# Two encoder layers on one core: the feed-forward of blocks 0 and 1 from group 8 on as seven products in place of eight, block 2 by itself

## The chip, the cores and the metric

The kernel is one program on one core of a Trainium2 chip. The core has five engines with a queue each, run in order: TensorE (PE: matmuls, with a second unit PEld that loads the weights of the next one), VectorE (DVE), ScalarE (ACT), GpSimd (POOL) and SyncE (SP), which here only issues DMAs. [...] The metric is the device time of one execution in microseconds (us): 2456.24 us in the median of three runs of the kernel before (2454.12 to 2459.05).

## The reference

Two layers of a streaming encoder on 1024 prompt tokens and 8 x 16 sample tokens, width 1024, all float32:

```python
for l in range(DEPTH):                       # 2 layers; prompt and sample tokens alike
    h = rms_norm(x, norm1_g[l])
    q, k, v, u = project(h, w_in[l], ...)    # u = a * sigmoid(b)
    a_o = attention in a window, with sinks  # 8 heads of 64, 2 kv heads
    c_o = silu(layer_norm(depthwise conv31(u)))
    x = x + concatenate([a_o * beta_a, c_o * beta_c]) @ w_out[l]
    h = rms_norm(x, norm2_g[l])
    x = x + square(relu(h @ w_up[l])) @ w_down[l]     # 1024 -> 4096 -> 1024
```

The last line is the feed-forward, and the change is in it.

## The kernel before, in words

**Blocks and products.** The 1152 tokens are three blocks of 384 columns. An activation x is held as 8 tiles of [128, 384] (features by tokens). Every product is done in float32r with both operands split into a high and a low part: of (w_hi + w_lo)(h_hi + h_lo) three of the four terms are summed, so a [1024, 128] weight unit times a block is 8 x 3 = 24 matmuls of 384 columns (`gemm`, L193 to L195). `half_unit` (L184 to L186) prepares half of a unit: a DMA of 256 KB into a `raw` buffer (4 of these), ScalarE casts the high part, and GpSimd subtracts it from the raw to get the low part; `w` has 6 buffers. A "step" below is 24 matmuls.

**Feed-forward.** The 4096 hidden features are 16 groups of 256. For a group and a block, "up" is 2 units, and `hidden` (L667 to L670) turns each of their results into relu, square, a high part (all three on ScalarE) and a low part (VectorE, L670). "Down" multiplies these by the group's rows of w_down: 8 results of [128, 384], 6 matmuls each (L686), each added to x by VectorE (L688). So a group costs one block 96 matmuls: 4 steps. `feed_forward` runs groups over several blocks, sharing the prepared weights; `feed_one` runs one block by itself, two groups at a time.

**The order of the work.** The program is traced in one order, and that order is the priority of the instructions for a list scheduler at build time: each engine's queue is fixed by it before the kernel runs. `side` streams (convolution, attention) give out a step or so beside each unit (`tick`), and one background stream `self.back` gives `mix` steps beside each unit (`unit_done`, `fill`); `flush` runs the rest of it.

**A layer.** After the projections, attention and convolution of the blocks, the order at the end of a layer (L833 to L850) is: groups up to `place` for blocks 0 and 1 in the foreground; then `out(2)` (the output projection of block 2, 8 units, and its norm) with groups `place` to `join` of blocks 0 and 1 as background; then the rest. In layer 0 `place` is 8 and `join` 16: blocks 0 and 1 do groups 8 to 15 beside and behind `out(2)`, and block 2 does all its 16 groups alone, as the background of layer 1's projections. In layer 1 `place` is 7 and `join` 8: from group 8 on the three blocks go together, and then block 2 does groups 0 to 7 alone at the very end. When a block's last group is done, its x is stored to DRAM and, in layer 0, its norm for layer 1 is computed (`stored`, `rmsnorm`, L230 to L248). Layer 1 begins with three background steps, then the first projection, which needs the norm of block 0.

**Buffers.** `big` has 9 slots of [128, 8 x 384] float32 for x, the two parts of h, the attention and convolution results and the like (`slot`, L77). PSUM: 3 banks `g` for products, 2 for the scores `s`, one each of `m`, `r` and `c`. `tmp` has 8 buffers of [128, 384].

The lines that matter most, by the profile's numbers: L184 to L186 weight preparation, L193 to L195 unit products, L212 to L248 the norm, L667 to L670 `hidden`, L686 and L688 `down`, L838 to L850 the end of a layer.

## Time and profile before

| | before |
|---|---|
| median of 3 runs | 2456.24 us |
| profiled execution, span | 2455.0 us |
| TensorE matmuls | 14206, busy 2397.7 us (98%) |
| VectorE | 2821 instructions, busy 1494.7 us (61%) |
| ScalarE | 2444, busy 1130.4 us (46%) |
| GpSimd | 1007, busy 1236.0 us (50%) |
| weight loads (`raw`) | 792 of 256 KB |

The profile is of one execution; its span runs from its first to its last instruction, and 2455.0 us is that execution's own time as the profile gives it, 1.2 us under the median of the timed runs. "Busy" of TensorE counts matmuls that overlap in a pipeline, so a matmul's own duration (0.34 us) is longer than the distance from its start to the next one's. A busy share is a mean over stages: VectorE is nearly always busy in the first 560 us, and has much idle time in the stages that the change touches. The time between an instruction's end and the next on its engine is laid to what released it ("<-").

### The profile page before, as it was taken

To read this page: it belongs to the slowest core of one execution; us is meant where nothing else is said; L and a number is where in the kernel's file an instruction comes from. 1 tells how busy PE (TensorE), PEld (TensorE's weight loads), DVE (VectorE), ACT (ScalarE), POOL (GpSimd) and SP (SyncE) were. 2 spreads that over 40 slices of the span, in tenths; PEclk is the share of its full clock that TensorE was granted. 3 is DMA by queue.
4 is the path that set the end of the run, shared out by engine and by line. 5 is a ranking of instruction groups with operands and counts; after the bars stand their busy time and mean duration, and the time that the engine had idled before them with its cause. 6 is when DMAs were issued, how large, how long until landed. Compare 5 with 4: busy or idle time off the path is not lost.

```text
span 2455.0 us, 38647 instructions
## 1 busy us (share of the span) xinstructions
PE 2397.7 (98%) x14206; PEld 2346.3 (96%) x14206; DVE 1494.7 (61%) x2821; ACT 1130.4 (46%) x2444; POOL 1236.0 (50%) x1007
## 2 busy tenths in 40 slices
PE   6999999999999999999999999999999999999999
PEld 6899888999999999999999999899999999999999
DVE  6999988996324333787777754889832433333322
ACT  5467545655333233544664566456433322222342
POOL 6875575566343233767755856756424422221363
PEclk9899999999999999999999999999999999999999
DMA  5423423333322222443333434334222211111342
GB/s 186 139 82 98 124 94 113 108 105 118 97 86 74 65 69 91 142 131 108 117 110 108 131 117 131 123 96 124 80 88 86 87 43 44 44 44 35 112 138 77
DMA packets 169692, 243.39 MB, mean 99 GB/s; under 512 B 23536, under 2 KB 70896, under 8 KB 169456
## 3 DMA queue, kind: packets, MB, share of 16 engines
q1 hardware_dynamic: 169504, 240.94, 31.4%
q8 instruction: 111, 1.82, 0.3%
q14 instruction: 77, 0.63, 0.1%
HBM read 230.27 MB, written 12.90 MB: 99 GB/s over the span
## 4 chain that ended last, share of the span: by engine, by line
PE 78%; DVE 15%; issue 2%; POOL 2%; ACT 2%; DMA 0%; SPq 0%; POOLq 0%; ACTq 0%; DVEq 0%
PE g L686 19%; PE g L193 15%; PE g L195 15%; PE g L194 15%; DVE c L318 6%; PE m L686 4%; PE r L686 4%; PE c L686 3%; PE s L496 1%; POOL w L186 1%; PE m L531 1%; DVE h L248 1%; DVE f L246 1%; DVE s L212 1%; DVE x L688 1%
## 5 line engine op out<-in xcount | busy, mean ns | idle before, releaser
L186 POOL TENSOR_TENSOR w<-raw,w 128x512 fp32r<-128x512 f32 x792 | 1051.6, 1339 | 1098.0 <-ACT w L185 1078.5
L185 ACT CAST w<-raw 128x512 fp32r<-128x512 f32 x792 | 483.1, 619 | 594.2 <-PE g L686 221.7
L193 PE MATMUL g<-h,w 128*128 128x384 f32 x2208 | 747.5, 339 | 7.1 <-ACT h L247 3.5
L195 PE MATMUL g<-h,w 128*128 128x384 f32 x2208 | 747.6, 339 | 0.0
L194 PE MATMUL g<-h,w 128*128 128x384 f32 x2208 | 746.1, 338 | 0.0
L686 PE MATMUL g<-hid,w 128*128 128x384 f32 x3072 | 566.1, 340 | 11.0 <-DVE x L688 8.4
L686 PEld LDWEIGHTS g<-hid,w 128*128 128x128 f32 x3072 | 535.2, 189 | 17.3 <-DVE x L688 10.4
L318 DVE SCALAR_TENSOR_TENSOR c<-u,vec,c 128x384 f32<-128x384 f32 (+1 forms) x960 | 498.0, 519 | 18.0
L193 PEld LDWEIGHTS g<-h,w 128*128 128x128 f32 x2208 | 417.4, 189 | 11.1 <-ACT h L247 4.3
L194 PEld LDWEIGHTS g<-h,w 128*128 128x128 f32 x2208 | 417.5, 189 | 1.4 <-issue 0.3
L195 PEld LDWEIGHTS g<-h,w 128*128 128x128 f32 x2208 | 417.6, 189 | 1.2 <-issue 0.2
L670 DVE TENSOR_TENSOR hid<-t,hid 128x384 fp32r<-128x384 f32 x192 | 141.4, 737 | 258.5 <-ACT hid L669 258.2
L688 DVE TENSOR_TENSOR x<-x,g 128x384 f32<-128x384 f32 x368 | 201.5, 552 | 159.1 <-PE g L686 158.4
L667 ACT ACTIVATE t<-g 128x384 f32<-128x384 f32 x192 | 94.3, 491 | 395.1 <-PE g L195 394.8
L688 DVE TENSOR_TENSOR x<-x,m 128x384 f32<-128x384 f32 x84 | 46.5, 554 | 196.7 <-PE m L686 196.7
L686 PE MATMUL m<-hid,w 128*128 128x384 f32 x576 | 117.8, 338 | 0.0
L686 PE MATMUL r<-hid,w 128*128 128x384 f32 x576 | 116.2, 335 | 0.0
L669 ACT CAST hid<-t 128x384 fp32r<-128x384 f32 x192 | 98.9, 515 | 11.5 <-PE r L686 6.9
L686 PEld LDWEIGHTS m<-hid,w 128*128 128x128 f32 x576 | 102.3, 188 | 0.3 <-DVE x L688 0.3
L668 ACT ACTIVATE t<-t 128x384 f32<-128x384 f32 x192 | 101.2, 527 | 1.9
L686 PEld LDWEIGHTS r<-hid,w 128*128 128x128 f32 x576 | 101.9, 188 | 0.0
L688 DVE TENSOR_TENSOR x<-x,r 128x384 f32<-128x384 f32 x84 | 46.5, 554 | 63.4 <-PE r L686 63.4
(150 smaller groups left out, 2519.2 us busy)
## 6 DMA issues: line engine op xcount, KB each, us to landing
raw<-in_w SPq DMA_DIRECT2D x792, 256.0 KB, 2.8
x<-in_x SPq DMA_DIRECT2D x24, 384.0 KB, 5.3
x<-xd SPq DMA_DIRECT2D x12, 384.0 KB, 5.4
xd<-x SPq DMA_DIRECT2D x4, 768.0 KB, 3.5
out_y<-x SPq DMA_DIRECT2D x4, 768.0 KB, 4.1
cs<-in_rope SPq DMA_DIRECT2D x6, 384.0 KB, 3.8
f<-in_ckv SPq DMA_DIRECT2D x8, 256.0 KB, 3.0
xd<-x SPq DMA_DIRECT2D x4, 384.0 KB, 3.6
```

Of the source, the lines that this page charges most:

```text
L185: nc.scalar.copy(u[:, 0], raw)
L186: nc.gpsimd.tensor_tensor(out=u[:, 1], in0=raw, in1=u[:, 0].bitcast(F32), op=ALU.subtract)
L193: nc.tensor.matmul(ps, lhsT=u(0, k), rhs=h(0, k), start=k == 0, stop=False)
L194: nc.tensor.matmul(ps, lhsT=u(0, k), rhs=h(1, k), start=False, stop=False)
L195: self.pe = nc.tensor.matmul(ps, lhsT=u(1, k), rhs=h(0, k), start=False, stop=k == KT - 1)
L318: t = nc.vector.scalar_tensor_tensor(out=o, in0=src(k), scalar=w, in1=o, op0=ALU.mult, op1=ALU.add)
L667: nc.scalar.activation(f, ps, AF.Relu)
L668: nc.scalar.activation(f, f, AF.Square)
L669: nc.scalar.copy(hid[:, 0], f)
L670: nc.vector.tensor_tensor(out=hid[:, 1], in0=f, in1=hid[:, 0].bitcast(F32), op=ALU.subtract)
L686: self.pe = nc.tensor.matmul(ps, lhsT=u(p), rhs=hid[:, q], start=i == 0, stop=i == n - 1)
L688: nc.vector.tensor_tensor(out=x[:, m], in0=x[:, m], in1=ps, op=ALU.add)
```

## The change

From group 8 on, blocks 0 and 1 do the feed-forward together as a 2 x 2 product of matrices: the weights of a group as four quarters A11 to A22, the activations as four quarters B11 to B22 (the two blocks, and the halves of the sum), and the four results from seven quarter products of sums of quarters, in the form with shared sums (S1 to S4 of the weights, T1 to T4 of the activations). All other groups stay as they were.

- `pair_forms`, once a layer: T1, T2 and T4 from the norms of blocks 0 and 1, each with a high and a low part, in three `big` slots; `last` overwrites part of block 1's norm with T3.
- `quad`: loads four quarters of weights (`raw`), S1 to S4 on VectorE, and `form`, which makes the high part (ScalarE) and the low part (GpSimd; VectorE for S3) of each of the seven.
- `pair_up`, once a group: 7 products of 12 matmuls into three `g` banks, with sums on VectorE between them, and then relu and square of the four quarters, their T sums, and the splits: seven tiles `hid`, 13 buffers.
- `pair_down`, once for two groups: two halves `mp` of 7 products; each product is 2 results of 6 matmuls, and each result is added to one x tile of one block.
- `out(2)` no longer computes block 2's norm; x of block 2 is stored to a DRAM buffer `kept`, and loaded and normed again (`second`) in the middle of the last `pair_down`. The norms of blocks 0 and 1 for layer 1 come after the whole stage (`done`).
- In layer 1 block 2 now does all 16 groups alone. `PLACE` falls by one in both layers.
- The PSUM banks `r`, `c`, `m` and `s`, the `hid` pool and others are given back for the stage, which has five banks `x` of its own; afterwards they are opened again. The columns of w_down are laid out in the order that the quarters want (`ROW`).

```diff
-JOIN = (16, 8)           # groups before block 2 joins, and
-PLACE = (8, 7)           # the group in which block 2 is ready
+PLACE = (7, 6)
+PAIR = (8, 8)
+NXW, NHF, NQ = 2, 13, 4
+ROW = (0, 2, 1, 3)
...
     def pr(self):
-        t = self.pp.tile([128, 512], F32, tag="r", name=self.nm("r"), bufs=1)
+        if self.aux is None:
+            return self.pg()
+        t = self.aux.tile([128, 512], F32, tag="r", name=self.nm("r"), bufs=1)
...
+    def parted(self, f, dst):
+        nc = self.nc
+        nc.scalar.copy(dst(0), f)
+        nc.vector.tensor_tensor(out=dst(1), in0=f, in1=dst(0).bitcast(F32), op=ALU.subtract)
+    def pair_forms(self, h0, h1):
+        nc = self.nc
+        F = lambda h, p, k: h(p, k).bitcast(F32)
+        T1, T2, T4 = (self.slot([2, 4, BT], F32R, "T") for _ in range(3))
+        sub, add = ALU.subtract, ALU.add
+        def op(eng, a, b, o):
+            t = self.tmp()
+            eng.tensor_tensor(out=t, in0=a, in1=b, op=o)
+            return t
+        for k in range(4):
+            d = op(nc.gpsimd, F(h1, 0, k), F(h0, 0, k), sub)
+            e = op(nc.gpsimd, F(h1, 1, k), F(h0, 1, k), sub)
+            t1 = op(nc.vector, d, e, add)
+            self.parted(t1, lambda p: T1[:, p, k])
+            d = op(nc.vector, F(h1, 0, 4 + k), t1, sub)
+            t2 = op(nc.vector, d, F(h1, 1, 4 + k), add)
+            self.parted(t2, lambda p: T2[:, p, k])
+            d = op(nc.gpsimd, F(h0, 0, 4 + k), t2, sub)
+            t4 = op(nc.vector, d, F(h0, 1, 4 + k), add)
+            self.parted(t4, lambda p: T4[:, p, k])
+        def last():
+            for k in range(4):
+                d = op(nc.gpsimd, F(h1, 0, 4 + k), F(h1, 0, k), sub)
+                e = op(nc.vector, F(h1, 1, 4 + k), F(h1, 1, k), sub)
+                self.parted(op(nc.vector, d, e, add), lambda p: h1(p, k))
+        part = lambda t: lambda p, k: t[:, p, k]
+        return {"B11": h0, "B21": lambda p, k: h0(p, 4 + k), "B22": lambda p, k: h1(p, 4 + k), "T3": h1,
+                "T1": part(T1), "T2": part(T2), "T4": part(T4)}, last
+    def quad(self, srcs):
+        nc = self.nc
+        A = []
+        for src in srcs:
+            raw = self.wp.tile([128, WK, 128], F32, tag="raw", name=self.nm("raw"), bufs=NRAW)
+            nc.sync.dma_start(raw if len(src.shape) == 3 else raw.rearrange("p (m j) c -> p m j c", m=2), src)
+            A.append(raw)
+        A11, A12, A21, A22 = A
+        def op(x, y, o):
+            t = self.xp.tile([128, WK, 128], F32, tag="S", name=self.nm("S"), bufs=4)
+            nc.vector.tensor_tensor(out=t, in0=x, in1=y, op=o)
+            return t
+        S1 = op(A21, A22, ALU.add)
+        S2 = op(S1, A11, ALU.subtract)
+        S3 = op(A11, A21, ALU.subtract)
+        S4 = op(A12, S2, ALU.subtract)
+        f = {"A11": A11, "S2": S2, "S1": S1, "S3": S3, "A12": A12, "S4": S4, "A22": A22}
+        def form(n):
+            own = n in ("S1", "A12")
+            u = (self.xp if own else self.wp).tile([128, 2, WK, 128], F32R, tag="w", name=self.nm("w"), bufs=NXW if own else NW)
+            nc.scalar.copy(u[:, 0], f[n])
+            eng = nc.vector if n == "S3" else nc.gpsimd
+            eng.tensor_tensor(out=u[:, 1], in0=f[n], in1=u[:, 0].bitcast(F32), op=ALU.subtract)
+            return u
+        return form
+    def pair_up(self, l, g, H, last=None):
+        nc, a = self.nc, self.a
+        half = lambda j, i: a["w"][l, 22 + 2 * g + j][:, WK * i:WK * i + WK]
+        form = self.quad([half(0, 0), half(0, 1), half(1, 0), half(1, 1)])
+        A, B, Z = (self.pg()[0] for _ in range(3))
+        def product(w, h, ps, start):
+            u = form(w)
+            for k in range(4):
+                for i, (p, q) in enumerate(((0, 0), (0, 1), (1, 0))):
+                    nc.tensor.matmul(ps, lhsT=u[:, p, k], rhs=H[h](q, k), start=start and k == 0 and i == 0, stop=k == 3 and i == 2, skip_group_check=True)
+        def q():
+            return self.xp.tile([128, BT], F32, tag="q", name=self.nm("q"), bufs=NQ)
+        def bank():
+            return self.px.tile([128, 512], F32, tag="x", name=self.nm("x"), bufs=5)[:, :BT]
+        def plus(o, t, ps):
+            nc.vector.tensor_tensor(out=o, in0=t, in1=ps, op=ALU.add)
+            return o
+        def hidden(src, t):
+            nc.scalar.activation(t, src, AF.Relu)
+            nc.scalar.activation(t, t, AF.Square)
+            return t
+        F = {}
+        def split(n, t):
+            u = self.xp.tile([128, 2, BT], F32R, tag="hid", name=self.nm("hid"), bufs=NHF)
+            self.parted(t, lambda p: u[:, p])
+            F[n] = u
+            return t
+        def less(x, y):
+            t = bank()
+            nc.vector.tensor_tensor(out=t, in0=x, in1=y, op=ALU.subtract)
+            return t
+        if last:
+            last()
+        product("A11", "B11", A, True)
+        c1 = self.tmp()
+        nc.scalar.copy(c1, A)
+        product("S2", "T2", B, True)
+        u2 = self.tmp()
+        nc.vector.tensor_tensor(out=u2, in0=c1, in1=B, op=ALU.add)
+        product("S1", "T1", Z, True)
+        product("S3", "T3", B, False)
+        u3 = self.tmp()
+        nc.vector.tensor_tensor(out=u3, in0=c1, in1=B, op=ALU.add)
+        b22 = plus(q(), u3, Z)
+        split("B22", hidden(b22, b22))
+        product("A12", "B21", A, False)
+        b11 = split("B11", hidden(A, q()))
+        product("S4", "B22", Z, False)
+        b12 = plus(bank(), u2, Z)
+        hidden(b12, b12)
+        t1 = split("T1", less(b12, b11))
+        split("T3", less(b22, b12))
+        t2 = split("T2", less(b22, t1))
+        product("A22", "T4", B, False)
+        b21 = plus(q(), c1, B)
+        split("B21", hidden(b21, b21))
+        split("T4", less(b21, t2))
+        return F
+    def pair_down(self, l, g, Fs, xs, mid=None):
+        nc = self.nc
+        w = self.w_down(l, g).rearrange("p (m j) c -> p m j c", j=4)
+        for mp in range(2):
+            form = self.quad([w[:, 4 * b + 2 * mp:4 * b + 2 * mp + 2, 2 * i:2 * i + 2] for b in range(2) for i in range(2)])
+            X, Z = ([self.px.tile([128, 512], F32, tag="x", name=self.nm("x"), bufs=5)[:, :BT] for _ in range(2)] for _ in range(2))
+            for wn, hn, ps, start, b, half in (("A11", "B11", X, True, 0, 0), ("S1", "T1", Z, True, 1, 1), ("S2", "T2", X, False, 1, 0),
+                                               ("S4", "B22", Z, False, 1, 0), ("S3", "T3", X, False, 1, 1), ("A12", "B21", None, True, 0, 0),
+                                               ("A22", "T4", X, False, 0, 1)):
+                u = form(wn)
+                for i in range(2):
+                    o = self.pg()[0] if ps is None else ps[i]
+                    n = 0
+                    for j in range(2):
+                        for p, q in ((0, 0), (0, 1), (1, 0)):
+                            nc.tensor.matmul(o, lhsT=u[:, p, 2 * i + j], rhs=Fs[j][hn][:, q], start=start and n == 0, stop=n == 5, skip_group_check=True)
+                            n += 1
+                    m = 4 * half + 2 * mp + i
+                    nc.vector.tensor_tensor(out=xs[b][:, m], in0=xs[b][:, m], in1=o, op=ALU.add)
+            if mid and mp == 0:
+                mid()
+    def pair_feed(self, l, groups, xs, forms, last, mid, done):
+        for g in groups[::2]:
+            Fs = [self.pair_up(l, g + j, forms, last if g == groups[0] and j == 0 else None) for j in range(2)]
+            self.pair_down(l, g, Fs, xs, mid if g == groups[-2] else None)
+        done()
...
+        early = ExitStack()
+        self.hp = early.enter_context(pool(name="hp0", bufs=4))
+        self.aux = early.enter_context(pool(name="aux0", bufs=1, space=PS))
...
-                h[b] = self.rmsnorm(x[b], l, G2)
+                if b < NB - 1:
+                    h[b] = self.rmsnorm(x[b], l, G2)
...
-            self.back, self.mix = self.feed_forward(l, range(place, join), [blk(b, join == NG) for b in range(2)]), mix[2]
+            self.back, self.mix = self.feed_forward(l, range(place, pair), [blk(b) for b in range(2)]), mix[2]
             out(2)
+            for i in range(0, KT, 4):
+                nc.sync.dma_start(kept[:, i:i + 4], x[2][:, i:i + 4])
+            forms, last = self.pair_forms(h[0], h[1])
             self.flush()
             self.mix = 0
-            with tc.tile_pool(name=f"fp{l}", bufs=NFW) as fp:
-                if join < NG:
-                    for _ in self.feed_forward(l, range(join, NG), [blk(0, True), blk(1, True), blk(2, join == 0)], True, fp):
+            early.close()
+            def second():
+                x[2] = self.load_x(kept, self.mark)
+                h[2] = self.rmsnorm(x[2], l, G2)
+            def done():
+                for b in range(2):
+                    for i in range(0, KT, 4):
+                        nc.sync.dma_start(nsrc[b][:, i:i + 4], x[b][:, i:i + 4])
+                    if not fin:
+                        nh.append(self.rmsnorm(x[b], l + 1, G1))
+            self.aux = None
+            with pool(name=f"xp{l}", bufs=1) as self.xp, pool(name=f"px{l}", bufs=1, space=PS) as self.px:
+                self.pair_feed(l, range(pair, NG), x, forms, last, second, done)
+            early = ExitStack()
+            self.hp = early.enter_context(pool(name=f"hp{l + 1}", bufs=4))
+            self.aux = early.enter_context(pool(name=f"aux{l + 1}", bufs=1, space=PS))
+            if fin:
+                with tc.tile_pool(name=f"fp{l}", bufs=NFW) as fp:
+                    for _ in self.feed_forward(l, range(NG), [blk(2, True)], True, fp):
                         pass
-                if fin:
-                    for _ in self.feed_forward(l, range(join), [blk(2, True)], True, fp):
-                        pass
-                else:
-                    self.back = self.feed_forward(l, range(join), [blk(2, True)])
+            else:
+                self.back = self.feed_forward(l, range(NG), [blk(2, True)])
```

## Rows read from the trace of the kernel before

**Rows 1.** The page, busy time of each engine, and TensorE's granted clock by slices.

```profile
PE 2397.7 (98%) x14206; PEld 2346.3 (96%) x14206; DVE 1494.7 (61%) x2821; ACT 1130.4 (46%) x2444; POOL 1236.0 (50%) x1007
PEclk9899999999999999999999999999999999999999
```

**Rows 2.** The page, the chain that ended last, by engine.

```profile
PE 78%; DVE 15%; issue 2%; POOL 2%; ACT 2%; DMA 0%; SPq 0%; POOLq 0%; ACTq 0%; DVEq 0%
```

**Rows 3.** Waits of TensorE: us in total, times, longest.

```profile
PE r L220 <- DVE f L239: 11.8, 2, 11.4
PE g L686 <- DVE x L688: 8.4, 5, 2.3
```

**Rows 4.** Windows: stretch, its us, busy us (instructions) by engine, clock, DMA.

```profile
590.00:670.00 80.00, 80.00 (x464) 79.69 (x463) 30.22 (x49) 34.84 (x65) 34.27 (x26) 1.00 0.33 105
745.00:970.00 225.00, 225.00 (x1302) 224.96 (x1301) 84.19 (x150) 76.34 (x144) 72.32 (x56) 1.00 0.22 66
1920.00:2300.00 380.00, 380.00 (x2174) 379.96 (x2175) 137.87 (x238) 104.00 (x201) 76.88 (x60) 1.00 0.15 45
2320.00:2440.00 120.00, 120.00 (x691) 119.93 (x689) 28.72 (x44) 51.81 (x97) 66.92 (x52) 1.00 0.34 106
```

**Rows 5.** Groups by shape, VectorE: count | busy us, mean ns | idle before.

```profile
L688 DVE TENSOR_TENSOR x<-x,g 128x384 f32<-128x384 f32 x368 | 201.5, 552 | 159.1 <-PE g L686 158.4
L670 DVE TENSOR_TENSOR hid<-t,hid 128x384 fp32r<-128x384 f32 x192 | 141.4, 737 | 258.5 <-ACT hid L669 258.2
L248 DVE TENSOR_TENSOR h<-f,h 128x768 fp32r<-128x768 f32 x48 | 60.0, 1258 | 2.1 <-ACT h L247 1.8
L246 DVE SCALAR_TENSOR_TENSOR f<-x,vec,r 128x384 f32<-128x384 f32 x96 | 53.6, 607 | 11.5 <-PE r L226 11.3
L256 DVE TENSOR_TENSOR t<-t,cs 128x384 f32<-128x384 f32 x30 | 28.7, 964 | 0.3
```

**Rows 6.** Timeline of VectorE around 2330: start, us, what ran.

```profile
2324.91 0.56 DVE L670 TENSOR_TENSOR hid<-t,hid 128x384 fp32r<-128x384 f32 x1 [1.59 <-ACT hid L669]
...
2333.30 1.74 DVE L670 TENSOR_TENSOR hid<-t,hid 128x384 fp32r<-128x384 f32 x1 [4.91 <-ACT hid L669]
...
2340.40 0.55 DVE L688 TENSOR_TENSOR x<-x,m 128x384 f32<-128x384 f32 x1 [2.56 <-PE m L686]
2340.87 0.55 DVE L688 TENSOR_TENSOR x<-x,r 128x384 f32<-128x384 f32 x1
```

**Rows 7.** Groups by shape, GpSimd.

```profile
L186 POOL TENSOR_TENSOR w<-raw,w 128x512 fp32r<-128x512 f32 x792 | 1051.6, 1339 | 1098.0 <-ACT w L185 1078.5 <-issue 6.8 <-PE g L195 4.3
L257 POOL TENSOR_TENSOR t<-t,cs 128x384 f32<-128x384 f32 x30 | 36.3, 1214 | 19.4 <-DVE t L255 12.1 <-issue 3.2 <-PE g L195 3.2
```

**Rows 8.** Groups by shape, ScalarE.

```profile
L185 ACT CAST w<-raw 128x512 fp32r<-128x512 f32 x792 | 483.1, 619 | 594.2 <-PE g L686 221.7 <-PE g L195 188.9 <-DMA raw<-in_w 46.4
L668 ACT ACTIVATE t<-t 128x384 f32<-128x384 f32 x192 | 101.2, 527 | 1.9
L669 ACT CAST hid<-t 128x384 fp32r<-128x384 f32 x192 | 98.9, 515 | 11.5 <-PE r L686 6.9
L667 ACT ACTIVATE t<-g 128x384 f32<-128x384 f32 x192 | 94.3, 491 | 395.1 <-PE g L195 394.8
```

**Rows 9.** Timeline of TensorE around 352, after a gap.

```profile
351.84 0.41 PE L193 MATMUL g<-ao,w 128*128 128x384 f32 x1 [3.06 <-DVE x L688]
...
353.35 0.52 PE L193 MATMUL g<-ao,w 128*128 128x384 f32 x1
353.67 0.52 PE L194 MATMUL g<-ao,w 128*128 128x384 f32 x1
```

**Rows 10.** Window with the lowest granted clock after the start.

```profile
350.00:400.00 50.00, 43.13 (x219) 39.24 (x219) 35.89 (x72) 20.92 (x38) 30.40 (x25) 0.86 0.35 110
```

**Rows 11.** Timeline of VectorE from the last addition of layer 0's out(2): its norm.

```profile
744.02 0.56 DVE L658 TENSOR_TENSOR x<-x,g 128x384 f32<-128x384 f32 x1 [3.63 <-PE g L195]
...
759.48 0.95 DVE L248 TENSOR_TENSOR h<-f,h 128x768 fp32r<-128x768 f32 x1
```

32 lines of the change are left out of this document (20 added, 12 removed).

## The prediction

> **What bounds the kernel now.** I read the page first. [...] The waits of TensorE come next: the two largest are 11.8 and 8.4 us in total [rows 3], so little is to be won by removing waits. Last, the windows, because the page's shares are means. In the stretches that the change replaces (745 to 970 us is the flush of layer 0's groups for blocks 0 and 1, 1920 to 2300 the same groups of layer 1 with block 2 among them) and in block 2's own (2320 to 2440), TensorE is busy for the whole of each window, and VectorE, ScalarE and GpSimd are at 20 to 56% [rows 4]. There the time is the number of matmuls times their distance: 805 us over 4631 matmuls in the four windows, 0.1738 us each. Twelve matmuls are then 2.09 us, a step of 24 is 4.17 us, 84 are 14.6 us.
>
> **What the change removes.** A group of blocks 0 and 1 costs 2 x 96 = 192 matmuls before. After it is 7 x 12 = 84 in the up part, and 2 x 7 x 12 = 168 for the down part of two groups, so 84 + 84 = 168. 24 fewer, in 8 groups and 2 layers: 384 matmuls, 384 x 0.1738 = 66.7 us. Two groups ("a pair") take 336 x 0.1738 = 58.4 us of TensorE in place of 66.7. Block 2's matmuls stay as many, since sharing a weight unit saves preparation and no matmul.
>
> **Added without a price.** Layer 1's block 2 now prepares its own weights for groups 8 to 15: 8 x 8 = 64 more loads, casts and subtractions. The stretch in which block 2 is alone before (from 2320 us) shows TensorE full with GpSimd at 66.92 of 120 us [rows 4]; that is the cover. The rate of loading in the pair stage stays near that of before: 8 loads for 14.6 + 14.6 us. `PLACE` brings out(2) forward by a group, 33 us; the first window shows VectorE from 590 us on at 30.22 of 80 us [rows 4], so block 2's attention and convolution are not late.
>
> **The pair stage.** VectorE per pair_up: 13 operations of 384 columns with an operand in PSUM (5 sums, 4 differences, 4 splits), 3 splits from SBUF alone, and 5 operations of 512 columns with two SBUF inputs (S1 to S4, the low part of S3). The first kind lasts 0.552 us, the same whatever GpSimd does, and back to back they follow each other in 0.47 us (2340.40, 2340.87) [rows 5, 6]. The second kind lasts 0.737 in the mean, 0.56 alone and up to 1.74 beside GpSimd [rows 5, 6]. 512 columns of that kind are not in the trace; between the means of 384 columns (0.737) and 768 (1.258) a line gives 0.91. Sum: 13 x 0.47 + 3 x 0.737 + 5 x 0.91 = 12.9 us beside 14.6 of TensorE. A half of pair_down: 14 x 0.47 + 5 x 0.91 = 11.1 us beside 14.6. A pair: 48.0 of 58.4 us, 82%; with 0.552 for the PSUM kind 52.4, 90%. GpSimd: 24 forms x 1.339 = 32.1 us, 55% [rows 7]. ScalarE: 28 casts x 0.619, 14 splits x 0.515, 8 quarters x (0.491 + 0.527), 2 copies of about 0.5: 33.7 us, 58% [rows 8]. So TensorE still has the longest sum, but VectorE has become a close second, and it sits between products: four or five of the seven go on summing in a bank that VectorE must have read first, with one product (2.09 us) of room. In pair_up u3 and b22, two operations in a row, must fit into the product A12; 0.55 + 0.47 leaves about 1 us. What stands ahead of them in VectorE's queue (an S sum that waits for a load, a split that waits for ScalarE) delays them, and TensorE with them. At the turn to pair_down T1 comes after b12, relu, square, a difference, a cast and a split, 0.55 + 1.02 + 0.55 + 0.52 + 0.55 = 3.2 us and the hand-overs, against 2 products, 4.2 us. And 14 `hid` tiles share 13 buffers: the last T4 waits until a tile has been used in both halves. Bounds per pair: 1 us (all fits) and 7 us (a lost wait of about 1 us at the turn, at T4 and in each of the four parts); I take 2 us, nearer to the rows of a VectorE that is not full: 8 pairs, 16 us.
>
> **The start of the stage.** Slots for T1 and T2 come free with the last matmul of out(2), since x, h of two blocks and the attention and convolution results fill the nine. In layer 0 what is left for TensorE then is 1 background step (8 steps beside 8 units) and the products A11, S2, S1: 4.2 + 3 x 2.09 = 10.4 us. S3 needs T3. Until T3 is there VectorE has 28 + 12 operations of 384 columns with two SBUF inputs and 5 of 512. From below, back to back: 40 x 0.47 + 5 x 0.6 = 21.8, a stall of 11 us. From above, if VectorE's and GpSimd's operations exclude each other wholly: 21.8 + 16 x 1.214 + 3 x 1.339 = 45.2, a stall of 35. With the mean of rows 5, less the overlap of 0.08, 40 x 0.66 + 4.6 = 31: a stall of 20 us; I take that, since GpSimd's share of the mean row is close to that of this stage. [...] In layer 1 `PLACE` 6 leaves 8 steps, 33 us of cover, with 10 us of VectorE's work in them: 31 + 10 against 44; I take 3 us, bounds 0 and 22.
>
> **The end of the stage.** `second` loads x of block 2 and norms it beside the last half of pair_down; then, in layer 0, the norms of blocks 0 and 1. From the last addition of x to the first pair of h tiles a norm takes 759.48 + 0.95 - 744.02 = 16.4 us [rows 11]; TensorE has 3 background steps, 12.5 us, so 4 us are bare. A norm is also some 13 us of VectorE (8 x 0.607, 4 x 1.258, four additions) in a half that has 3 us to spare. In layer 0 I take 6 in all (bounds 0 and 14), in layer 1 3 (0 and 10). SP's queue is in order, so the stores of `done` and the gated load of `second` hold back the weight loads behind them; with 4 `raw` and 6 `w` buffers ahead that is hidden.
>
> **Sum.** 66.7 saved; 20 + 4 and 3 at the starts, 6 and 3 at the ends, 16 inside: 52. Net 14.7 us: 2455.0 - 14.7 = 2440.3 by the profiled execution; the median is 1.2 us above it: 2441 us.
>
> [...] The rows show that an operation with one PSUM input keeps 0.552 us and one with two SBUF inputs goes from 0.56 to 1.74 us [rows 5, 6]: the excess, 1.18, is nearly a whole subtraction of GpSimd (1.339). [...]
>
> **The rivals.**
> - *Nearly all is hidden.* The scheduler fills the queues so that a pair loses 1 us, and the starts cost their lower bounds (11 and 0) with 3 at one end: 22 us lost, 2455.0 - 44.7 + 1.2 = 2412. For it: full windows next to 20 to 56% of the other engines; against: no row shows TensorE waiting so often on VectorE without a loss. Chance 0.16.
> - *VectorE paces the pair stage* (slower). Of a pair's 26 operations with two SBUF inputs each waits 0.8 us in place of the mean row's 0.18: 48.0 + 16 = 64 us, over TensorE's 58.4, and a pair then loses 6.2 us, 50 in all. 66.7 - 50 - 36 = -19: 2476 us. It decides from the point where a pair loses (66.7 - 36) / 8 = 3.8 us. For it: L256, which mostly runs beside GpSimd, lasts 0.964 [rows 5]; against: L670's mean of 0.737, with GpSimd at 50%. Chance 0.23.
> - *Start and end by the sum of both engines* (slower): 35 + 4 and 22 at the starts, 14 and 10 at the ends, 16 inside: 101 lost, 2490 us. For it the 1.74 us row; against it the same mean. Chance 0.10.
> - [...] Chance 0.09.
>
> **How the numbers follow.** The forecast, 2441, has 0.42, and its own range is 2425 to 2453. 0.2% is 5 us, about what a measurement of this kernel tells from no change. Faster: the first rival's 0.16 and 0.38 of the forecast's, 0.54. Within 0.2%: the last rival's 0.09 and 0.02 of the forecast's, 0.11. Slower: the second and third rivals with the last 0.02 of the forecast's, 0.35. The range goes from the first rival to just short of the third, 2410 to 2487: 0.08 lies below it and 0.10 above.
>
> **What would show it.** 13822 matmul records, 384 fewer, a few missing. Right: windows inside the stage with TensorE over 95%, and a gap of some 20 us with a lower clock behind it where layer 0's pair stage begins, and a small one in layer 1. A wait of TensorE on VectorE's sums of more than 30 us in total inside the pairs, or a busy VectorE of over 95% there, would speak for the second rival; gaps of over 30 us at the starts for the third. The prediction is wrong if the pairs take over 62 us each, or if the starts and ends together cost less than 20 us or more than 60.

## The result, and the profile after

The kernel with the change takes **2539.32 us** (median, 2537.03 to 2540.59) against 2455.73 (2454.12 to 2459.05) for the kernel before in the same runs: ratio 1.0335, 95% interval 1.0321 to 1.0349. It is 83.6 us slower. The forecast was 2441, and the time lies above the range.

The page of after: busy time by engine, the granted clock by slices, and the chain that ended last.

```profile
PE 2374.0 (94%) x13822; PEld 2304.8 (91%) x13822; DVE 1719.5 (68%) x3189; ACT 1264.5 (50%) x2700; POOL 1456.0 (57%) x1167
PEclk9999989999989999899999999999999899999999
PE 64%; DVE 20%; issue 6%; POOL 5%; ACT 3%; DMA 2%; SPq 0%; DVEq 0%; POOLq 0%; ACTq 0%
```

Against [rows 1] there are 384 matmul records fewer, as counted, and TensorE is busy for 23.7 us less in a span that is 83.8 us longer. Against [rows 2] TensorE's share of the chain went from 78 to 64%, VectorE's from 15 to 20, GpSimd's from 2 to 5. So the work was saved, and more than was saved was paid back in waits. All but the norm's are new beside [rows 3] (waits of TensorE: us in total, times, longest; L944 is pair_down's products, L870 pair_up's, L700 the flush, L234 a norm):

```profile
PE x L944 <- DVE x L897: 21.7, 14, 3.7
PE g L234 <- DVE f L253: 17.8, 2, 14.4
PE g L870 <- ACT t L904: 14.4, 2, 13.7
PE g L700 <- ACT t L681: 14.4, 1, 14.4
PE g L870 <- DVE t L911: 14.3, 10, 3.9
```

Windows of after, with the columns of [rows 4]. In order: a stretch ahead of the change; layer 0's first sums; its first pair; its second and third pair; its last pair; the flush of layer 1; block 2 alone.

```profile
590.00:670.00 80.00, 80.00 (x463) 79.59 (x462) 30.60 (x47) 34.93 (x64) 37.07 (x28) 1.00 0.35 112
721.00:752.00 31.00, 9.69 (x39) 8.09 (x38) 29.70 (x35) 10.69 (x20) 21.85 (x16) 0.68 0.16 52
721.10:805.30 84.20, 58.90 (x295) 56.09 (x295) 65.48 (x99) 37.43 (x72) 45.35 (x34) 0.84 0.18 55
805.00:934.00 129.00, 121.15 (x668) 118.42 (x667) 88.83 (x160) 61.95 (x119) 65.33 (x48) 0.97 0.20 64
935.20:1015.40 80.20, 72.42 (x389) 70.18 (x387) 60.38 (x109) 40.91 (x73) 36.80 (x28) 0.94 0.29 93
1936.00:1993.00 57.00, 38.22 (x194) 36.74 (x193) 40.82 (x61) 15.69 (x32) 24.79 (x20) 0.82 0.11 36
2320.00:2440.00 120.00, 120.00 (x692) 120.00 (x691) 30.28 (x46) 53.01 (x99) 75.30 (x60) 1.00 0.43 130
```

The stretches that the change doesn't touch are as full as before, and block 2 alone hides its new preparation. The stage loses at its starts, at the end of layer 0, and some in every pair. In the middle pairs VectorE is busy for 88.83 of 129 us, 69%: it isn't full, and TensorE waits for it all the same.

**Where the time went.** A pair is timed from its first matmul to the next pair's first. At that point 42 of its own matmuls, 7.3 us, are still to run, among the next pair's (805 to 817 us). So a middle pair's stretch holds its full 336 matmuls, 58.4 us without a loss; the first pair's only 294, 51.1 us; the last pair's, timed to its last product, 378, 65.7 us (the counts of the windows above have one or two more from across their edges, and nine small ones of a norm in the last). In layer 0 the four take 84.2, 65.0, 65.0 and 79.8 us, and then 42.7 us go by to layer 1's first result; in layer 1 the flush takes 56.9 us (eight steps, 33.4 without a loss) and the pairs 64.8, 65.3, 65.0 and 84.3, the last with 33 matmuls of block 2. A pair loses 6.6 us by itself. From the end of out(2) to layer 1's first result it was 257.5 us before and is 340.7, with as much due (a group moved in, a group's worth saved): 83.2 lost. Of that the pairs are 26.4, the start 84.2 - 51.1 - 6.6 = 26.5, the end the other 30.3. Layer 1 went from 542.2 to 602.9: 60.7 lost, 30.6 at the start (23.5 in the flush, 64.8 - 51.1 - 6.6 = 7.1 in the first pair), 26.4 in the pairs, 3.7 at the end. Together 143.9 where 52 were forecast; 143.9 - 66.7 is 77 of the 84 us. The other 6.5 lie ahead of the change: out(2) of layer 0 ended 26.9 us earlier in place of 33.4. Executions of all these kernels differ by as much there (out(1) of layer 0 ended between 441.6 and 449.7 us).

**The four places, each in its rows.** First the turn from pair_up to pair_down, TensorE's timeline of after (start, us, what ran; idle before and its releaser in brackets), and then its clock there:

```profile
839.61 2.36 PE L870 MATMUL g<-T,w 128*128 128x384 f32 x12 [0.70 <-DVE t L911]
...
843.74 0.86 PE L870 MATMUL g<-h,w 128*128 128x384 f32 x4
844.43 0.68 PE L944 MATMUL g<-hid,w 128*128 128x384 f32 x3
847.32 1.38 PE L944 MATMUL x<-hid,w 128*128 128x384 f32 x6 [2.21 <-DVE x L897]
849.03 3.29 PE L944 MATMUL x<-hid,w 128*128 128x384 f32 x10 [0.33 <-DVE x L897]
```

```profile
848.50:851.50 3.00, 2.67 (x9) 2.47 (x9) 3.00 (x8) 1.04 (x3) 0.00 (x0) 0.50 0.02 5
```

TensorE stands for 2.21 us until a difference (L897) has freed a bank, runs six matmuls, stands for another 0.33, and then runs ten in 3.29 us, where twelve at a granted clock of 1.00 take 2.25 (11 x 0.1738 + 0.34): the granted clock was 0.50 for some 3 us, half of that lost besides. With waits of 0.74 and 0.70 us ahead of A22 in the two pair_up these gaps are 4.0 of the 6.6 us, and the clock some 1.5. VectorE's timeline of after shows why: the sum for b12 starts at 844.63, right behind S4's product; the difference comes 1.6 us later, behind relu and square.

```profile
839.01 0.54 DVE L911 TENSOR_TENSOR t<-t,g 128x384 f32<-128x384 f32 x1
...
839.95 0.54 DVE L879 TENSOR_TENSOR q<-t,g 128x384 f32<-128x384 f32 x1
...
844.63 0.56 DVE L879 TENSOR_TENSOR x<-t,g 128x384 f32<-128x384 f32 x1 [1.13 <-PE g L870]
846.24 0.57 DVE L897 TENSOR_TENSOR x<-x,q 128x384 f32<-128x384 f32 x1 [1.05 <-ACT x L884]
846.72 0.55 DVE L897 TENSOR_TENSOR x<-q,x 128x384 f32<-128x384 f32 x1
```

The scheduler had put A22's product (839.61) ahead of S4's (its end is the row at 843.74). A22 adds to the bank that u3 (L911) reads, S4 to the one that b22 (L879) reads, one sum later: A22 could run first. So nothing was left beside that chain.

Second, the start of layer 1. ScalarE's timeline of after:

```profile
1964.33 0.51 ACT L790 CAST T<-t 128x384 fp32r<-128x384 f32 x1 [1.23 <-DVE t L802]
1965.94 0.51 ACT L790 CAST T<-t 128x384 fp32r<-128x384 f32 x1 [1.09 <-DVE t L802]
1966.36 1.25 ACT L681 ACTIVATE t<-g 128x384 f32<-128x384 f32 x3
```

The relu (L681) of a flush step stands in the queue behind casts that wait for VectorE's sums; at 1966.36 it does three in a row, late ones: TensorE had ended their products by 1952.51, and from 1953.21 on ScalarE stood idle for 10.2 us in all, each time ahead of a cast. TensorE had waited 14.4 us for it (the fourth wait above). In layer 0's first pair the 13.7 us on L904, also ScalarE, begin in the same way: the copy of c1 (751.04) stands behind two casts of T3 that wait for VectorE. But there the order holds back one product only, A12's: the next, S3's, needs T3 itself, whose last cast starts at 752.03.

Third, the end of layer 0, TensorE's timeline of after:

```profile
1018.84 1.23 PE L234 MATMUL g<-cst,f 128*128 128x1 f32 x6 [3.46 <-DVE f L253]
1021.84 0.90 PE L240 MATMUL g<-cst,s 128*128 128x128 f32 x3 [1.77 <-DVE s L228]
1037.10 1.44 PE L234 MATMUL g<-cst,f 128*128 128x1 f32 x6 [14.36 <-DVE f L253]
1038.40 0.67 PE L207 MATMUL g<-h,w 128*128 128x384 f32 x1
```

Block 2's steps (L207) were there to cover the norms, but the small matmuls of both norms (the rows x6, x3 and x6) stand ahead of them.

Fourth, the first sums. While GpSimd works on them too, most of VectorE's T sums and their splits take 1.3 to 1.6 us, then 0.55 (its timeline of after):

```profile
738.55 1.34 DVE L802 TENSOR_TENSOR t<-t,h 128x384 f32<-128x384 f32 x1
739.82 1.62 DVE L802 TENSOR_TENSOR t<-h 128x384 f32<-128x384 f32 x1
...
749.10 0.55 DVE L802 TENSOR_TENSOR t<-h 128x384 f32<-128x384 f32 x1
```

### The profile page after: what moved, and what is told of

Read it like the earlier page. It is cut to its first block, busy times and chain, and to the rows that moved or that the text cites. A ratio compares the mean times of both kernels' runs of the same rounds, so it can differ in the third digit from the quotient of the medians.

```text
span 2538.8 us, 38948 instructions
## 1 busy us (share of the span) xinstructions
PE 2374.0 (94%) x13822; PEld 2304.8 (91%) x13822; DVE 1719.5 (68%) x3189; ACT 1264.5 (50%) x2700; POOL 1456.0 (57%) x1167
## 3 DMA queue, kind: packets, MB, share of 16 engines
q1 hardware_dynamic: 164064, 264.01, 33.4%
## 4 chain that ended last, share of the span: by engine, by line
PE 64%; DVE 20%; issue 6%; POOL 5%; ACT 3%; DMA 2%; SPq 0%; DVEq 0%; POOLq 0%; ACTq 0%
PE g L700 12%; PE g L207 11%; PE g L208 10%; PE g L209 10%; PE x L944 8%; DVE c L332 6%; POOL w L854 3%; PE g L870 2%; PE m L700 2%; PE r L700 2%; DMA raw<-in_w 2%; PE s L510 1%; DVE S L840 1%; PE c L700 1%; PE g L944 1%
## 5 line engine op out<-in xcount | busy, mean ns | idle before, releaser
L207 PE MATMUL g<-h,w 128*128 128x384 f32 x1696 | 576.9, 341 | 7.2 <-ACT h L261 3.5
L209 PE MATMUL g<-h,w 128*128 128x384 f32 x1696 | 575.7, 340 | 0.0
L208 PE MATMUL g<-h,w 128*128 128x384 f32 x1696 | 574.7, 339 | 0.0
L700 PE MATMUL g<-hid,w 128*128 128x384 f32 x2304 | 435.1, 343 | 30.2 <-ACT t L681 14.4
L700 PEld LDWEIGHTS g<-hid,w 128*128 128x128 f32 x2304 | 404.2, 191 | 38.6 <-ACT t L681 14.7
L207 PEld LDWEIGHTS g<-h,w 128*128 128x128 f32 x1696 | 322.0, 190 | 11.3 <-ACT h L261 4.3
L208 PEld LDWEIGHTS g<-h,w 128*128 128x128 f32 x1696 | 321.8, 190 | 1.4 <-issue 0.3
L209 PEld LDWEIGHTS g<-h,w 128*128 128x128 f32 x1696 | 321.7, 190 | 1.4 <-POOL w L200 0.2
L944 PE MATMUL x<-hid,w 128*128 128x384 f32 x1152 | 234.8, 353 | 21.8 <-DVE x L897 21.7
L944 PEld LDWEIGHTS x<-hid,w 128*128 128x128 f32 x1152 | 213.5, 199 | 27.5 <-DVE x L897 26.4
L854 POOL TENSOR_TENSOR w<-S,w 128x512 fp32r<-128x512 f32 x96 | 134.4, 1406 | 156.2 <-ACT w L852 147.6
L852 ACT CAST w<-S 128x512 fp32r<-128x512 f32 x128 | 78.1, 620 | 164.2 <-PE x L944 70.4
L870 PE MATMUL g<-h,w 128*128 128x384 f32 x768 | 145.2, 340 | 15.2 <-ACT t L904 14.4
L870 PEld LDWEIGHTS g<-h,w 128*128 128x128 f32 x768 | 136.6, 191 | 16.2 <-ACT t L904 15.1
L947 DVE TENSOR_TENSOR x<-x,x 128x384 f32<-128x384 f32 x192 | 102.2, 550 | 67.0 <-PE x L944 66.5
L870 PE MATMUL g<-T,w 128*128 128x384 f32 x576 | 116.4, 352 | 26.4 <-DVE t L911 14.3
```

The source lines that it names most:

```text
L207: nc.tensor.matmul(ps, lhsT=u(0, k), rhs=h(0, k), start=k == 0, stop=False)
L208: nc.tensor.matmul(ps, lhsT=u(0, k), rhs=h(1, k), start=False, stop=False)
L209: self.pe = nc.tensor.matmul(ps, lhsT=u(1, k), rhs=h(0, k), start=False, stop=k == KT - 1)
L700: self.pe = nc.tensor.matmul(ps, lhsT=u(p), rhs=hid[:, q], start=i == 0, stop=i == n - 1)
L854: eng.tensor_tensor(out=u[:, 1], in0=f[n], in1=u[:, 0].bitcast(F32), op=ALU.subtract)
L870: nc.tensor.matmul(ps, lhsT=u[:, p, k], rhs=H[h](q, k), start=start and k == 0 and i == 0, stop=k == 3 and i == 2, skip_group_check=True)
```

## The experiments

Each run's marks, read from its timeline, in us. "Pairs" are layer 0's second and third; "end" is its last pair and what follows to layer 1's first result; the last two columns are layer 1's flush (from out(2) to its first product) and its first pair. Without a loss "first" would read 51.1, "pairs" 58.4, "end" 65.7 + 16.7 (three steps of block 2 and one unit; 25 us more where six steps come first), and the last two 33.4 (66.7 where block 2 is due after five groups, 166.8 in "two pairs") and 51.1.

```
run                 time     ratio [95%]             first  pairs        end          flush  first
after              2539.32  1.0335 [1.0321, 1.0349]  84.2  65.0  65.0  79.8 + 42.7    56.9  64.8
flush first        2539.29  1.0338 [1.0320, 1.0355]  84.4  65.0  64.9  79.8 + 42.7    34.0  88.1
interleaved        2509.35  1.0213 [1.0197, 1.0229]  73.4  64.9  64.6  76.2 + 42.5    35.8  73.7
steps first        2509.56  1.0220 [1.0205, 1.0236]  84.6  65.1  65.0  84.8 + 37.4    57.2  65.2
S4 before A22      2532.69  1.0315 [1.0299, 1.0331]  84.5  64.0  64.1  79.1 + 42.5    57.1  65.1
no sums            2478.05  1.0082 [1.0067, 1.0097]  66.8  64.7  64.8  72.8 + 42.8    33.1  64.6
no low part        2524.43  1.0275 [1.0259, 1.0290]  72.6  67.0  65.9  79.0 + 42.7    57.1  57.1
sums in SBUF       2552.32  1.0385 [1.0368, 1.0403]  89.8  66.0  68.0  78.0 + 42.2    57.4  70.3
three              2513.77  1.0226 [1.0210, 1.0241]  78.9  68.4  68.1  83.6 + 36.5    35.9  78.7
in order           2521.04  1.0255 [1.0235, 1.0274]  85.4  62.3  64.9  74.9 + 42.7    57.6  62.3
deferred           2536.63  1.0317 [1.0299, 1.0335]  84.0  64.9  65.0  79.6 + 42.8    56.9  64.6
starts and ends    2491.44  1.0131 [1.0110, 1.0151]  74.9  64.8  64.8  84.1 + 37.4    35.8  73.7
combination        2473.36  1.0065 [1.0050, 1.0080]  68.9  62.2  63.4  80.1 + 38.0    35.8  74.3
  5 groups         2484.92  1.0114 [1.0099, 1.0129]  64.8  62.2  62.3  79.1 + 38.0    68.7  63.8
  4 alone, 5       2470.22  1.0061 [1.0046, 1.0076]  63.0  62.3  63.3  80.5 + 38.0    68.7  64.6
  6 and 5          2459.48  1.0013 [1.0003, 1.0022]  68.8  62.3  62.9  80.3 + 38.0    68.6  63.1
two pairs          2520.12  1.0252 [1.0235, 1.0269]  65.2     -     -  79.0 + 42.7   187.9  64.1
```

**Flush first.** The flush is issued ahead of the sums.

```
+            self.flush()
+            self.mix = 0
             forms, last = self.pair_forms(h[0], h[1])
-            self.flush()
-            self.mix = 0
```

> The sums T (pair_forms) are traced behind the flush of the background steps, nothing else. [...] Layer 0 has one step left and stays. 2515 to 2527 us. Theory B (VectorE and GpSimd exclude each other, their sum is the time): what the flush gains the first pair loses, 2535 to 2545 us.

The range of 2515 to 2527 missed, and B's number, 2535 to 2545, came out. The rows show another reason than B's. The 14.4 us wait is gone and the first product comes 23 us sooner, but the pair behind it is 23 us longer. GpSimd's queue has the flush's weight subtractions ahead of the sums now, and one stands idle for 9.11 us behind a cast that itself waits until TensorE has used up a weight buffer; GpSimd's first sums start at 1951.93. Its timeline in this run:

```profile
1946.52 1.29 POOL L200 TENSOR_TENSOR w<-raw,w 128x512 fp32r<-128x512 f32 x1 [9.11 <-ACT w L199]
```

Either order is a loss; the next run puts the steps between the sums.

**Interleaved.** Block 2 is ready a group earlier in layer 0, and two steps go beside each quarter of the sums.

```
-PLACE = (7, 6)
+PLACE = (6, 6)
...
             self.parted(t4, lambda p: T4[:, p, k])
+            self.fill(2)
```

> PLACE (6, 6), so that layer 0 too has eight steps left at the start of the stage, and two of these steps are traced behind each quarter of the T sums. Theory A (order of the queues): relus and casts, weight subtractions and sums take turns, the steps cover the sums: the two starts lose 10 to 20 us in place of 49, 2505 to 2518 us. Theory B (VectorE's and GpSimd's operations are simply added): layer 0 gains at most 8 us, 2528 to 2540 us.

A holds: 30 us, and both flushes are within 3 us of their work (nine steps in layer 0, 37.6 of 40.1 us, eight in layer 1). The first pairs, 73.4 and 73.7 us, still lose 22 each.

**Steps first.** Six steps of block 2 ahead of the norms of blocks 0 and 1.

```
-                    if not fin:
-                        nh.append(self.rmsnorm(x[b], l + 1, G1))
...
                 self.back = self.feed_forward(l, range(NG), [blk(2, True)])
+                self.fill(6)
+                for b in range(2):
+                    nh.append(self.rmsnorm(x[b], l + 1, G1))
```

> Six steps of block 2 are traced ahead of the two norms at the end of layer 0. [...] Theory B: the norms are VectorE work that has to be done first anyhow: 2533 to 2543 us.

B fails: 2509.56 lies 23 us under its range. The end has 25 us more of block 2's work in it (six steps in place of none ahead of the norms) and is no longer. TensorE is full there (window of this run):

```profile
1003.00:1050.00 47.00, 47.00 (x275) 46.96 (x274) 34.40 (x49) 26.45 (x45) 34.27 (x26) 1.00 0.51 180
```

**S4 before A22.** In product():

```
+                    if w == "A22":
+                        self.after(mm, self.s4)
+                    if w == "S4":
+                        self.s4 = mm
```

> Product A22 is held behind product S4 on TensorE (an order for the scheduler, no wait), in all 16 groups. [...] Theory B: the pair is as long as VectorE's and GpSimd's work: 2533 to 2543 us.

Just under B: 2532.69, and 4.7 of the 6.6 us won lie ahead of the change. Pairs are 64.0 us in layer 0 and 65.1 to 65.4 in layer 1. The gap of 2.21 us became one of 1.06 and the slow stretch behind it went, but another of 1.61 us came up ahead of it (TensorE's timeline of this run): a product of pair_down, which the scheduler had put between, waits for ScalarE.

```profile
836.57 0.78 PE L948 MATMUL g<-hid,w 128*128 128x384 f32 x3 [1.61 <-ACT q L887]
...
843.12 2.43 PE L948 MATMUL x<-hid,w 128*128 128x384 f32 x12 [1.06 <-DVE x L901]
```

**In order.** All seven products keep the code's order.

```
-            eng = nc.vector if n == "S3" else nc.gpsimd
+            eng = nc.gpsimd
...
+                    if before is not None:
+                        self.after(mm, before)
+                    self.last_up = mm
```

> All seven products of pair_up stand on TensorE in the order in which the code has them (A11, S2, S1, S3, A12, S4, A22), and the low part of S3 is taken on GpSimd like that of the other six, so that S3 isn't late. Theory A (the pairs lose 6.6 us each because the scheduler put A22 and A12 ahead of S4 and S3, so the chain b12, relu, square, difference has no product beside it): the gaps of .74, .70, 2.2 and .33 us and the slow stretch go, a pair takes 60 to 61.5 us, 2505 to 2515 us in all. Theory B (VectorE's chain is too long for any order): the gaps move to the products that are now held, pairs stay at 64 to 66 us, 2530 to 2545 us.

Between the two, nearer to A: pairs of 62.3 to 64.9 us, 18 us in all. At the turn 0.76 us is left, and the next twelve matmuls take 2.42 us, against 2.25 at a granted clock of 1.00 (TensorE's timeline and a window of this run):

```profile
842.39 2.42 PE L949 MATMUL x<-hid,w 128*128 128x384 f32 x12 [0.76 <-DVE x L902]
```

```profile
784.00:909.00 125.00, 118.42 (x655) 115.41 (x656) 87.20 (x147) 60.91 (x119) 75.90 (x56) 0.99 0.21 68
```

VectorE is busy for as long, 87.20 us of two pairs. It no longer has S3's eight low parts (7.0 us), but its twelve splits from SBUF take twice as long beside GpSimd (rows of two pairs, after and this run), and the pairs are shorter all the same:

```profile
L791 DVE TENSOR_TENSOR hid<-q,hid 128x384 fp32r<-128x384 f32 x12 | 6.3, 557 | 0.0
L791 DVE TENSOR_TENSOR hid<-q,hid 128x384 fp32r<-128x384 f32 x12 | 12.7, 1062 | 9.8 <-ACT hid L790 9.8
```

Layer 0's third pair, 64.9 us, shows how else a pair loses: an S sum waits for its weights' load, u2 (L912) stands behind it in VectorE's queue, and TensorE behind u2; the granted clock was 0.66 in the 5 us from 895. The prediction had named such a sum. VectorE's timeline of this run, then TensorE's:

```profile
890.97 0.69 DVE L840 TENSOR_TENSOR S<-raw,raw 128x512 f32<-128x512 f32 x1 [0.95 <-DMA raw<-in_w]
...
894.65 0.55 DVE L912 TENSOR_TENSOR t<-t,g 128x384 f32<-128x384 f32 x1
895.25 4.98 PE L872 MATMUL g<-h,w 128*128 128x384 f32 x18 [1.83 <-DVE t L912]
```

The two parts of this edit weren't run apart; the next run has nothing of S3's low part on VectorE either, without the order, and its pairs didn't shorten.

**No low part** and **no sums**, each a suspected cost taken away:

```
-            eng.tensor_tensor(out=u[:, 1], in0=f[n], in1=u[:, 0].bitcast(F32), op=ALU.subtract)
+            nc.gpsimd.memset(u[:, 1].bitcast(F32), 0.0)
```

> The low parts of the weights in the pair stage are zeros written by GpSimd in place of a subtraction (their products are computed with zeros, so the low part of the weights is left out there; S3's too). GpSimd then reads nothing in the stage. Theory A: VectorE's splits and sums lose their waits for GpSimd, some 1 us a pair, and the order stays: pairs of 63 to 65 us, 2525 to 2540 us. Theory B: pairs of 59 to 60 us and a start shorter by half: 2485 to 2505 us.

```
+        return {"B11": h0, "B21": up, "B22": lambda p, k: h1(p, 4 + k), "T3": h1, "T1": h0, "T2": up, "T4": h1}, last
```

> All T sums are left out, T1 to T4 read h as it is (so the results of the stage are other numbers); products, weights and the sums behind the products stay. It prices the starts. Both theories: layer 0's first pair falls from 84 to 66 us and layer 1's wait of 14.4 us on a relu goes, 42 to 50 us less in all, 2489 to 2497 us; pairs stay at 65 us. If the starts cost less than 30 us here, the loss lies elsewhere than I read it.

In "no low part" GpSimd reads no weights. Contention is gone from the middle pairs, where S's last sum takes 0.69 us in place of 0.95, and they are 1 to 2 us longer: TensorE's gap at the turn is 3.65 us now. So the pairs' loss isn't contention. Layer 0's first pair is 11.6 us shorter and layer 1's 7.7; that much of the starts is contention and GpSimd's shorter queue together. "No sums" leaves out all T sums, and 61 us go: the first pair is 66.8 us, layer 1's flush takes its 33.1, and the last pairs are 7 us shorter. With three big buffers free, block 2 is loaded and its norm begins at 713 us already, beside the first pair; that this is what the last pair wins wasn't shown apart. The middle pairs stay at 64.7. Even without sums the first pairs lose 7 to 9 us more than a later one. "No low part" came out at the edge of A, "no sums" lower than expected.

**Sums in SBUF** and **deferred**, two other ways to relieve the turn: the differences for T3 and T4 go to SBUF in place of a bank, or behind the second group's u3 and b22.

```
-            t = bank()
+            t = self.tmp() if own else bank()
```

> The differences for T3 and T4 behind each pair_up go to an SBUF buffer in place of one of the five x banks. [...] Theory A2 (chain): the sums for T1 are late anyhow, the gap moves to the second product: pairs of 64 to 65, 2530 to 2540 us. [...]

```
+        if before:
+            before()
         split("B22", hidden(b22, b22))
```

> The differences for T3 and T4 and the splits of the first group of a pair are issued behind u3 and b22 of the second group, so that the second group's sums stand ahead of them on VectorE. Theory A (the wait is one of order in VectorE's queue): the gap at u3 (.74 + .70 us) goes, the turn stays at 2.2 us: pairs 63 to 64 us, 2520 to 2530 us. Theory B (the deferred work is only moved and then stands ahead of c1 or of the first quarter of pair_down, and holds two more banks meanwhile): pairs 65 to 68 us, 2538 to 2560 us.

The first is 13 us slower, above A2's range. The turn's gaps do fall under 1 us, but u2 of the next pair_up is late: VectorE's queue has splits and sums of S ahead of it, the last of them 1.75 us long, and TensorE stands 2.1 us (VectorE's timeline of this run):

```profile
832.95 1.75 DVE L840 TENSOR_TENSOR S<-raw,S 128x512 f32<-128x512 f32 x1
834.62 0.54 DVE L907 TENSOR_TENSOR t<-t,g 128x384 f32<-128x384 f32 x1
```

The second changes nothing: pairs of 65 us, 2.21 us at the turn, a time just below B's range and far from A's.

**Three** is "interleaved", "steps first" and "sums in SBUF"; **starts and ends** the first two of them.

> Three edits at once: the T sums interleaved with PLACE (6, 6), the differences for T3 and T4 in SBUF, and six steps of block 2 ahead of the two norms (2509.6 alone). Theory A1: the gains add up, 2509 - 30 - 28 = 2440 to 2462 us, level with the kernel before. A2: 2475 to 2490. Theory B: 2500 to 2515 us.

> The two edits that won 30 us each when done alone, together: block 2 ready a group earlier in layer 0 with two background steps beside each quarter of the sums, and six background steps ahead of the two norms at the end of layer 0. Theory A (they act at different places, and add): 2475 to 2485 us. Theory B (block 2's steps that cover the end are those that the other edit already used): 2495 to 2510 us.

The third edit takes back what the others won. The two alone win 48 us, not 60: by the marks of the single runs layer 0's start gives 8, layer 1's 12 and the end 25, which is 45. What the single runs won beyond that lay mostly ahead of the change (out(2) of layer 0 ended 3.3 us sooner in "steps first" and 5.5 in "interleaved", its group's 33.4 taken out), and 3.8 us at the end of "interleaved".

**Combination** is "starts and ends" with "in order"; under it three variants of when block 2 is due. PLACE (5, 5), with four steps beside each quarter, does group 5 of layer 0 twice for both blocks, since a block by itself takes two groups at a time (ALONE (5, 4) comes to the same and gave 2485.32, 1.0120 [1.0100, 1.0139]); ALONE (4, 4) does it once; PLACE (6, 5) leaves layer 0 alone.

> The edits that won at the starts (block 2 a group earlier in layer 0, two background steps beside each quarter of the sums), at the end of layer 0 (six steps ahead of the norms) and inside the pairs (the code's order of products on TensorE, S3's low part on GpSimd), together. Theory A (three separate places, the losses add): 2491 - 18 = 2473, 2468 to 2478 us; pairs 62.3 us. Theory B (with the starts covered VectorE has no slack left over and the order costs it): pairs 64 us or more, 2482 to 2495 us.

> As the combination, with block 2 ready after five groups in both layers, so that 8 more background steps are left in each layer, and four of them beside each quarter of the sums. Theory A (what is left at the starts, 15 us in each first pair, is TensorE with nothing to do while the sums run): both first pairs fall to 62 to 66 us, 2440 to 2458 us in all. Theory B (the first pair is long because VectorE and GpSimd are still at work on the sums whatever TensorE has, or block 2 is late when it is due so early): 2465 to 2490 us.

> The combination with block 2 ready after five groups in both layers (block 0 alone for five groups in layer 0 too, so that no group is done twice, as group 5 was in the run before, 33.4 us of work too many) and four background steps beside each quarter of the sums. Theory A (the starts were bare for want of work on TensorE, and 2484.9 less 33.4 is what is left): first pairs 63 to 66 us, 2446 to 2456 us, level with the kernel before or up to 0.4% faster. Theory B (block 2's attention and convolution are late when it is due another group earlier in layer 0): out(2) is followed by gaps and moves less than 33 us, 2460 to 2475 us.

> As the two runs with PLACE (5, 5), in which a block by itself takes two groups at a time, so that group 5 of layer 0 was done twice for both blocks (33.4 us of work too many); here both blocks have four groups by themselves in both layers, and none is done twice. Theory A (the starts were bare for want of work on TensorE; 2485 less 33.4 is what is left): out(2) of layer 0 ends 33 us earlier, first pairs 63 to 66 us, 2446 to 2457 us, level with the kernel before. Theory B (block 2's attention and convolution are late when due so early, since block 0 has eight steps fewer beside them): gaps ahead of out(2) in layer 0, 2460 to 2475 us.

> The combination with block 2 ready after five groups in layer 1 alone, with four background steps beside each quarter of the sums there; layer 0 as in the combination (six groups, two steps). Theory A (want of work beside the sums): layer 1's first pair falls from 74.3 to 64 us, layer 0's stays at 69: 2473 less 10, 2460 to 2466 us. Theory B (the steps only move the wait into the flush): the time from out(2) to the end of the first pair, less the 33.4 us of the added group, stays at 110 us, 2470 to 2476 us.

The combination meets A: three places, and they add. With enough steps the first pairs fall to 63 to 65 us, so the starts were bare of work (A), though the first pairs still lose 12 to 14 us over their 51.1; but due after four groups alone block 2 itself is late: out(2) of layer 0 moves forward by 23.3 us of the 33.4 (B; 2470). Done in layer 1 only it gives **2459.48 us**, the best version: 0.13% above before, within the 0.2% that the prediction counted as no change, though its interval, 1.0003 to 1.0022, lies on the slower side. Windows of it: layer 0's first pair and layer 1's.

```profile
717.00:779.00 62.00, 49.98 (x258) 47.13 (x257) 47.80 (x74) 31.94 (x64) 39.68 (x28) 0.92 0.20 64
1917.00:1980.00 63.00, 55.55 (x296) 53.23 (x295) 44.47 (x73) 31.94 (x63) 41.33 (x30) 0.95 0.22 68
```

**Two pairs.** The kernel after with PAIR = (12, 12).

> The kernel after with two pairs a layer in place of four (groups 12 to 15), the other groups as before, in the flush, which then has 32 or more steps left beside the sums in both layers. Theory A (the losses are mostly per layer, at the ends and at the start for want of cover, and a pair by itself wins 1.7 us): the start of layer 0 is covered, four pairs win 7 us, the ends still cost 37 and 11, and layer 1's start up to 23: 2455 + 41 to 64 = 2496 to 2522 us. Theory B (the losses come with every pair): half of the 84 us, 2495 to 2500, with the stage's starts as long as in the kernel after: first pair of layer 0 over 80 us.

A. With 32 steps of flush layer 0's first pair is 65.2 us, and its end costs what it did. Layer 1 loses nearly as much as before, 21 us: 188 us for 40 steps of 4.17. TensorE's timeline of this run shows the same wait, at the same place in the queue, with work in plenty behind it:

```profile
1950.94 2.29 PE L700 MATMUL g<-hid,w 128*128 128x384 f32 x6 [15.41 <-ACT t L681]
```

## Why the prediction was wrong

- **What the change removes, and what it adds without a price:** right. 384 records fewer, block 2 alone fully covered, out(2) earlier by a group in both layers.
- **The pair stage, 2 us a pair: failed at the turn.** It set "3.2 us and the hand-overs, against 2 products, 4.2 us" and went by the code's order. The queue had A22 ahead of S4, the chain had no product beside it, and a pair lost 6.6 us, near the 7 that were its upper bound. Held in order it loses 3.9 to 6.5. The amounts of work were near: x<-x,g 550 ns against 552, the splits from SBUF 609 against 737, S sums 0.71 to 0.99 us against 0.91, and VectorE 44.9 us a pair (89.73 for two) against 48.0.
- **The start of layer 0, 24 us: the size about right, 26.5,** beyond its 51.1 us of work and a pair's own 6.6. No run shows the sum's 4 us as such; after shows in their place 22 matmuls that came 0.32 us apart between 729 and 756 us, at a granted clock of 0.50, 3.2 us more than at 0.1738. "No sums" takes 17.4 of it away. For the other 9 the prediction had no term, and what they are wasn't tried apart: a later pair has 42 matmuls of the pair before among its first ones, the first pair has none. Some 11.6 go with GpSimd's weight subtractions ("no low part"). In the start VectorE's T sums took 1.34 and 1.62 us while GpSimd worked on them too, and 0.55 behind it; the pairs, which didn't shorten in "no low part", show that this isn't what bounds them.
- **The start of layer 1, 3 us: failed, 30.6,** 23.5 of it in the flush. "31 + 10 against 44" compared sums of work. The steps that were to cover the sums go through ScalarE, and their relus stood behind the sums' casts. "Two pairs" shows it apart from the amount of cover.
- **The ends, 6 and 3: failed in layer 0, 30.3.** "TensorE has 3 background steps, 12.5 us, so 4 us are bare" had the steps beside the norms; they stood behind them. "Steps first" shows it: 25 us won. Layer 1's 3.7 is as forecast. SP's queue held its order: the load of `second` waited from 959.37 to 962.56, and two weight loads went out right behind it, at 964.43 and 964.92.
- **The rivals.** The second had a pair's loss right (6.2 us) for a wrong reason: VectorE is at 69%, and "in order" shortened the pairs with VectorE busy for as long. The sign that the prediction set for this rival, over 30 us of waits on VectorE's sums, came all the same (21.7 on L897, 14.3 on L911, starts and last pairs among them): such a wait told of the order, not of a full engine. The third had the size of the starts and ends (91 lost with the pairs' own taken out, where it had 85), but contention is only a part of that, at most 11.6 and 7.7 us of the two starts. The last, within 0.2%, missed: the ratio is 1.0335. A granted clock of 0.50 was there, as some 1.5 us of the pair's loss.
- **By its own tests** it was wrong at "the pairs take over 62 us each", and the starts and ends together cost 91 us, where more than 60 was to show it wrong.

The rows at 1966.36 and 834.62 are two cases of an instruction behind a late one in its engine's queue: three relus whose products had ended by 1952.51, directly behind a cast that started at 1965.94, and u2, whose product had ended by 833.12, directly behind a sum of 1.75 us. The three failed terms have one error in common: work was counted as cover without its place in the queue. At the start of layer 1 and the end of layer 0 it stood behind what it was to cover; at the turn, A22 had run before the chain began.

What stays open: the 3.9 us that a pair still loses at best in order, the 7 to 9 us of the first pairs, the last pairs (80.1 us in layer 0 of the combination, where 378 matmuls and 29 of block 2 are 70.7), and whether the order or S3's move carried "in order".

## What to carry to other kernels

Before a stretch of one engine's work is counted as cover, follow it through every queue that it passes: here relus behind late casts cost TensorE 14.4 us, though ScalarE was busy for only 15.69 of 57 us in layer 1's flush, and a norm's small matmuls ahead of ready steps cost 14.36. Fillers go between the pieces of what they cover, and ahead of what waits. Where a saving of one matmul in eight puts a second engine between them, the order in which the scheduler has issued them is worth a good part of the saving: here up to 2.7 of the 8.3 us that a pair was to save.

## What was not expected of the hardware

Gaps of 2.04 to 2.21 us between full products, with a second of 0.21 to 0.79 us just behind, were followed by a stretch of some 3 us at a granted clock of 0.50, in the first three pairs of both layers of after. At the same place, gaps of 0.76 us ("in order") and 1.06 us ("S4 before A22") were not. A gap of 1.83 us in "in order" (895.25) was followed by one, a gap of 1.87 us in "combination" (881.75) was not (granted clock 1.00 from 881 to 886): in these runs the length of a gap doesn't tell it alone. After the 14.36 us gap matmuls came 0.32 us apart for 4.6 us (1038.40 to 1043.02; the granted clock was 0.50 from 1019 to 1043).
